# Queries and keys of a sparse-attention layer turned unsplit, compressed probabilities of two heads in one transpose, score matmuls over 512 columns

## The chip, the cores and the metric

One core of a Trainium2 chip runs the whole kernel. The metric is the device time of one execution in microseconds (us); the figure for a kernel is the median of several runs. Engines are called as in the profile: PE is the matrix engine, PEld its weight loads, DVE the vector engine, ACT the scalar engine, POOL GpSimd, SP the engine that here only issues transfers.

## What is computed

A decoder layer over 512 tokens of width 1024: a normed input is projected to pooling channels, 8 query heads of 64, six key/value slots for 2 groups, and gates. The attention part, in the reference's terms, is for each query head:

```python
s = einsum('bqgrd,bngd->bgrqn', q, kc) * scale        # 31 compressed blocks
p_cmp = masked_softmax(s, cmp_end <= t, -1);  o_cmp = p_cmp @ vc
s = einsum('bqgrd,bgqkld->bgrqkl', q, ksel) * scale   # selected blocks (all 8 of 8 here)
o_sel = masked_softmax(s, ...) @ vsel
s = einsum('bqgrd,bkgd->bgrqk', q, kw) * scale        # window of 512
o_win = masked_softmax(s, ...) @ vw
o = g0 * o_cmp + g1 * o_sel + g2 * o_win
```

q and the keys are normed and rotated first. The pooled and the attention outputs are projected, gated, added to the input, and a gated conv-MLP of inner width 2816 follows. All in float32.

## The kernel before

**Split numbers.** To keep float32 accuracy, an operand is split into a high part (float32r, written by ACT) and a low part (the rest, a DVE subtraction), in `split` (L424), and products are made as high*high + high*low + low*high. For queries and keys the two parts lie on the 128 partitions, 64 rows each: one matmul over 128 rows adds two of the products, and two matmuls, with the key tile `KT[0, ...]` and `KT[1, ...]`, add all four.

**A planner sets the order.** Every instruction is noted in a `Plan` with a price, and `emit` (L374) replays the notes in an order found by a list scheduler: up to 12 tries, of which the one with the least modelled time is written out. Each engine then works through its list in that fixed order. PE has two streams: `m` (attention) and `f` (projections of pooling channels and gates, `feature`, L705), and takes from `f` when `m` has nothing ready. `pl.behind(op)` only delays the planner's start of an operation until `op` is done; it is no wait on the chip. SBUF pages of 128x512 come from one pool of `PAGES` (L51). PSUM has 2 banks `mm` (stream f), 3 banks `tr`, one `av`, one double one `sc`.

**Turning q and k.** `rope_split(t)` (L653) rotates the 8 query heads and the 4 key heads (2 branches x 2 groups) of token block t (128 tokens), and splits them: `qs` holds, per head, 64 high and 64 low columns; `ks` holds the key's high part twice (`ks[0]`) and its low part twice (`ks[1]`). `qk_transpose(t)` (L678) turns each head's 128x128 tile on PE: 8 transposes for q and 8 for k per block, in groups of four to a PSUM bank, and ACT copies each bank to `QT` or `KT` as float32r. `turned[t]` (L700) is the last operation of block t; the rotation of block t+2, the loads of `w1` (L806) and `poolw`, and the clearing of `kcz` and `PZ` are put behind it.

**Scores.** `scores(h, i)` (L912): for query block i of head h and each key block j up to i, two matmuls of 256 columns (two branches x 128 keys).

**Compressed branch.** `cmp_scores` (L870) uses a block-diagonal `kcz` as the fixed operand and 512 columns of `QT`. `cmp_softmax` (L880) leaves `cst`: per head and block 32 high, 32 low and 32 high columns (96). `cmp_transpose(g, i)` (L901) turns the four heads of a group for block i, 4 transposes per call, 8 calls, and ACT copies 96 rows to `PTc`. `av` (L959) multiplies with `vst`, 96 rows x 64.

**Afterwards.** `PTc`'s and `cst`'s memory is taken over in the MLP by the tiles `th` (`tt`, `t2`, L1079). The MLP's 18 calls of `up_fast` (L1209) load weights (`r`), make low parts by an accumulating transfer from POOL (`sl`, `split_by_dma`, L1084), and multiply.

Of the kernel before, what the change touches and what calls it, by code (L numbers as in the profile page):

```python
# [9 lines left out]
F32R = mybir.dt.float32r  # L10
# [37 lines left out]
    CST[_n] = (_o, _o + _w)  # L48
    _o += _w
NCST = _o  # L50
PAGES = 54  # L51
RINGS = {"wraw": 3, "whi": 3, "wlo": 3}
PLAIN = 4
DIRECT = (0, 3)
# [342 lines left out]
def hybrid_layer(ctx: ExitStack, tc: tile.TileContext, xT, pos, par, cst, poolw, w1, wa, wb, wf,  # L397
# [9 lines left out]
    def f32(ap):  # L407
        return ap.bitcast(F32)

    def page(name, shape=(P, T), dt=F32):  # L410
        return pl.tile(sb, shape, dt, name, "pg", PAGES)

# [5 lines left out]
    def keep(name, shape, dt=F32, bufs=1):  # L418
        return pl.tile(sb, shape, dt, name, "t_" + name, bufs)
# [55 lines left out]
    def C(n):  # L475
        return cs[:, CST[n][0]:CST[n][1]]
# [142 lines left out]
    for t in range(NT):  # L619
# [11 lines left out]
        with pl.behind(sines):  # L631
# [2 lines left out]
                                 op1=ALU.subtract)  # L634
        vv[t] = v
    b_done = pl.last()
    vg = keep("vg", (P, H, NT))
    DVE.tensor_scalar(gates, gates, 1.0, 0.5, op0=ALU.add, op1=ALU.mult)
    DVE.tensor_mul(vg, gates[:, :, 0::3].rearrange("p t h -> p h t"),
                   C("valid")[:, None, :].to_broadcast([P, H, NT]))  # L640

    def rope_on(x, tmp, idx, n):
        np_ = x.shape[0]
# [4 lines left out]
        DVE.tensor_mul(x[:, :, 0:16], x[:, :, 0:16], ct[:, None, :].to_broadcast([np_, n, 16]))  # L648
        DVE.tensor_add(x[:, :, 0:16], x[:, :, 0:16], tmp)

    qsp, ksp = [], []

    def rope_split(t):  # L653
        x, y = qp[t], kp[t]
        DVE.tensor_mul(x[:, :, 0:16], x[:, :, 0:16], gq[:, None, :].to_broadcast([P, 8, 16]))
        y4 = y.rearrange("p (b g) d -> p b g d", b=2)
        DVE.tensor_mul(y4, y4, gkv[:, 1:3][:, :, None, :].to_broadcast([P, 2, 2, DH]))
        tmp = page("rt", (P, 12, 16))
        rope_on(x, tmp[:, 0:8], t, 8)
        rope_on(y, tmp[:, 8:12], t, 4)  # L660
        qs = [page("qs", (P, 4, 2, DH), F32R) for _ in range(2)]
        ks = [page("ks", (P, 4, 2, DH), F32R) for _ in range(2)]
        for g in range(2):
            split(qs[g][:, :, 0], qs[g][:, :, 1], x[:, 4 * g:4 * g + 4])
        kx = y[:, :, None, :].to_broadcast([P, 4, 2, DH])
        split(ks[0], ks[1], kx)
        qsp.append(qs)
        ksp.append(ks)

    for t in range(NT):  # L670
        x, y = qp[t], kp[t]
# [3 lines left out]
    pl.span = [pl.last().i, 0]  # L675
    QT, KT = {}, {}

    def qk_transpose(t):  # L678
        for g in range(2):
            pt = bank("tr", (P, 4, P))  # L680
            with pl.unit():
                for i in range(4):
                    PE.transpose(pt[:, i], f32(qsp[t][g][:, i].rearrange("p a d -> p (a d)")), ident)
            QT[g, t] = page("qt", (P, 4, P), F32R)
            ACT.activation(QT[g, t], pt, AF.Copy)
        for s in range(2):
            pt = bank("tr", (P, 2, 2, P))
            with pl.unit():
                for g in range(2):
                    for b in range(2):  # L690
                        PE.transpose(pt[:, g, b], f32(ksp[t][s][:, 2 * b + g].rearrange("p a d -> p (a d)")), ident)
            KT[s, t] = page("kt", (P, 2, 2, P), F32R)
            ACT.activation(KT[s, t], pt, AF.Copy)

    rope_split(0)
    rope_split(1)
    turned = []
    for t in range(NT):
        qk_transpose(t)
        turned.append(pl.last())  # L700
        if t + 2 < NT:
            with pl.behind(turned[t]):
                rope_split(t + 2)

    def feature(i, hi, lo):  # L705
        wh, wl = weights(flat(wf[i]), 1024)
# [136 lines left out]
        for z in kcz.values():  # L843
            POOL.memset(f32(z), 0.0)
    pk = compress_out(1)
    vst = keep("vst", (96, 2, DH), F32R)
    for g in range(2):
        src = pk[g * 32:(g + 1) * 32, 0:64]
        for s in range(2):
            ACT.activation(vst[s * 32:(s + 1) * 32, g], src, AF.Copy, scale=0.5)  # L850
        DVE.scalar_tensor_tensor(vst[64:96, g], src, 0.5, f32(vst[g * 32:(g + 1) * 32, g]),
                                 op0=ALU.mult, op1=ALU.subtract)

    def compress_kt():
        pt = bank("tr")
# [9 lines left out]
                               AF.Copy)  # L865

    cps, cst_ = {}, {}
    PTc = {g: pl.tile(sb, (96, 4, T), F32R, "ptc", "ptc", 1) for g in range(2)}

    def cmp_scores(g):  # L870
        pt = bank("tr")
        for i in range(NT):
            with pl.unit():
                for s in range(2):
                    PE.matmul(pt, kcz[s, g][:, i], QT[g, i].rearrange("p a b -> p (a b)"), start=(i == 0 and s == 0),
                              stop=(i == 3 and s == 1))
        cps[g] = page("cs", (P, 4, P))
        ACT.activation(cps[g].rearrange("p a b -> p (a b)"), pt, AF.Copy)

    def cmp_softmax(g):  # L880
        pt = bank("tr", (P, 4, P))
        with pl.unit():
            for hh in range(4):
                PE.transpose(pt[:, hh], cps[g][:, hh], ident)
        e = page("ce", (P, 16, 32))
        e4 = e.rearrange("p (h t) n -> p h (t n)", h=4)
        sm = keep("csm", (P, 3, 16), bufs=2)
        st = cst_[g] = keep("cst", (P, 16, 3, 32), F32R)
        DVE.tensor_add(e4, pt, C("cmask")[:, None, :].to_broadcast([P, 4, P]))
        DVE.tensor_reduce(sm[:, 0], e, axis=AX, op=ALU.min)  # L890
        DVE.tensor_sub(e, e, sm[:, 0][:, :, None].to_broadcast([P, 16, 32]))
        ACT.activation(e, e, AF.Exp, scale=-1.0)
        DVE.tensor_reduce(sm[:, 1], e, axis=AX, op=ALU.add)
        DVE.reciprocal(sm[:, 2], sm[:, 1])
        DVE.tensor_mul(sm[:, 2], sm[:, 2], vg[:, 4 * g:4 * g + 4].rearrange("p h t -> p (h t)"))
        DVE.tensor_mul(e, e, sm[:, 2][:, :, None].to_broadcast([P, 16, 32]))
        ACT.activation(st[:, :, 0], e, AF.Copy)
        ACT.activation(st[:, :, 2], e, AF.Copy)
        DVE.tensor_sub(st[:, :, 1], e, f32(st[:, :, 0]))

    def cmp_transpose(g, i):  # L901
        pt = bank("tr", (P, 4, P))
        with pl.unit():
            for hh in range(4):
                PE.transpose(pt[0:96, hh], f32(cst_[g][:, 4 * hh + i].rearrange("p a n -> p (a n)")), ident)
        ACT.activation(PTc[g][:, :, i * P:(i + 1) * P], pt[0:96], AF.Copy)

    Pt, PT, po, Oraw = {}, {}, {}, {}
    Oh = [page("oh", dt=F32R) for _ in range(4)]
# [2 lines left out]
    def scores(h, i):  # L912
        g, hh = divmod(h, 4)
        n = i + 1
        pt = bank("sc", (P, 4, 2, P)) if n > 2 else bank("tr", (P, 2, 2, P))
        with pl.unit():
            for j in range(n):
                for s in range(2):
                    PE.matmul(pt[:, j], QT[g, i][:, hh], KT[s, j][:, g], start=(s == 0 and j % 2 == 0),
                              stop=(s == 1), skip_group_check=True)  # L920
        sm = keep("asm", (P, 4, 2), bufs=4)
        if n > 2:
            pp = [pl.tile(sb, (P, T), F32, "pp", "pp", 10)[:, :n * P].rearrange("p (j k) -> p j k", k=P) for _ in range(2)]
        else:
            x = pl.tile(sb, (P, T), F32, "pp", "pp", 10).rearrange("p (b j k) -> p b j k", b=2, k=P)
            pp = [x[:, b, :n] for b in range(2)]
        for b in range(2):
            DVE.tensor_tensor_reduce(out=pp[b], in0=pt[:, 0:n, b], in1=mask[:, NT - n:NT], scale=1.0,
                                     scalar=3.0e38, op0=ALU.add, op1=ALU.min, accum_out=sm[:, 0, b:b + 1])
        for b in range(2):  # L930
            ACT.activation(pp[b], pp[b], AF.Exp, bias=sm[:, 0, b:b + 1], scale=-1.0,
                           accum_out=sm[:, 1, b:b + 1])
        DVE.reciprocal(sm[:, 2], sm[:, 1])
        DVE.tensor_mul(sm[:, 3], sm[:, 2], gates[:, i, 3 * h + 1:3 * h + 3])
        for b in range(2):
            DVE.tensor_scalar_mul(pp[b], pp[b], sm[:, 3, b:b + 1])
            Pt[h, b, i] = pp[b]
# [21 lines left out]
    def av(h, b):  # L959
# [4 lines left out]
        o = po[h]  # L964
        parts = [(0, 0, 0, 0), (1, 0, 1, 128), (2, 256, 2, 256), (2, 0, 3, 256)]
        if b == 1:
            PE.matmul(o[0:64], vst[:, g], PTc[g][:, h % 4], start=False, stop=False)
            parts = parts[::-1]
        for r, s, j, t0 in parts:
            n = 512 - t0  # L970
# [29 lines left out]
    cmp_softmax(0)  # L1000
    scores(0, 2)
    scores(0, 3)
    extra = {(0, 2 * i + 2): (lambda i=i: cmp_transpose(0, i)) for i in range(NT)}
    extra.update({(4, 2 * i): (lambda i=i: cmp_transpose(1, i)) for i in range(NT)})
    extra[2, 6] = lambda: cmp_softmax(1)
    for h in range(H):
        def nxt(i):
# [68 lines left out]
    H2 = T // 2  # L1076
    nh, nl, th, tl = {}, {}, {}, {}
    yh, yl = [None] * KF, [None] * KF
    tt = pl.tile(sb, (P, 4, T), F32R, "th", "ptc", 1)  # L1079
    t2 = pl.tile(sb, (P, 3, T), F32R, "th", "t_cst", 1)  # L1080
    t3 = [pl.tile(sb, (P, T), F32R, n, "t_" + n, 1) for n in ("oraw", "ot")]
    b11 = [[pl.tile(sb, (P, T), F32R, "nh", "pt", 6) for _ in range(2)] for _ in range(2)]

# [5 lines left out]
    def halves(k):  # L1089
# [13 lines left out]
        DVE.tensor_sub(tb[:, :H2], b2[:, H2:], b1[:, H2:])  # L1103
        DVE.scalar_tensor_tensor(tb[:, H2:], ta[:, H2:], -1.0, b2[:, :H2], op0=ALU.mult, op1=ALU.subtract)
        for i, x in ((0, ta), (1, tb)):
            th[k, i] = tt[:, k] if i == 0 else t2[:, k] if k < 3 else t3[0]
            tl[k, i] = page("tl", dt=F32R) if k or i else t3[1]
            (split_by_dma if i else split)(th[k, i], tl[k, i], x)

# [282 lines left out]
```

## Time and profile before

| | |
|---|---|
| time, median of 3 runs | 702.31 us (701.93 to 702.53) |
| span of the profiled execution, first to last instruction | 700.4 us |
| its own time | not listed; its span lies 1.9 us under the median of the runs |
| PE busy | 693.4 us, 4142 matmuls |
| DVE, ACT, POOL busy | 479.5, 433.4, 103.3 us |

"Busy" is the union of the instructions' spans. A matmul's span holds a pipeline tail of some 0.16 us (a 512-column one is 0.39 us long while the next one starts 0.23 us after it), so the cost of one matmul in a row of them is the distance between starts, not the span. Almost every line of the profile is L393, the line that replays the notes, so operations are told apart by the tiles they write and read: `tr<-cs,qs` is a transpose into a `tr` bank of the tile `qs` with the identity in `cs`.

### The profile page before, as it was taken

Reading aid. Unit: us, or ns where it says so; the run is one execution under the profiler, and the core shown is the slowest. Engines: PE = TensorE matmul, PEld = TensorE weight load, DVE = VectorE, ACT = ScalarE, POOL = GpSimd, SP = SyncE. Lnnn points to the kernel's source line nnn. Section 1 sums busy time; section 2 is a strip of 40 time slices with the busy share of each in tenths; the row PEclk is TensorE's granted clock in tenths of the full one; section 3 lists DMA queues with packets and bytes.
Section 4 is the critical chain, followed back from the end, with each engine's and each line's share of the span. In section 5 each row is a group of like instructions: output and inputs, shape, how many; then the busy total and the mean of one; then the engine's idle time right before and its main releaser. Section 6 shows DMA issues by size and latency. Waiting matters only on the chain.

```text
span 700.4 us, 11319 instructions
## 1 busy us (share of the span) xinstructions
PE 693.4 (99%) x4142; PEld 612.7 (87%) x4142; DVE 479.5 (68%) x1024; ACT 433.4 (62%) x792; POOL 103.3 (15%) x127
## 2 busy tenths in 40 slices
PE   9999999999999999999999999999999999999997
PEld 8898888888888888888888898999999999999986
DVE  6768488777866653685559876776777867675542
ACT  8567378766776663343358766776776766675320
POOL 0011310010011010000012232222322222121000
PEclk9999999999999999999999999999999999999999
DMA  8468342555565557844468887897787887774131
GB/s 296 141 162 246 89 121 76 135 140 131 122 166 146 156 128 204 306 159 139 159 140 201 191 175 172 203 208 181 176 177 185 192 207 187 178 177 104 45 129 60
DMA packets 45271, 113.99 MB, mean 163 GB/s; under 512 B 5280, under 2 KB 5408, under 8 KB 45216
## 3 DMA queue, kind: packets, MB, share of 16 engines
q1 hardware_dynamic: 29232, 76.57, 33.9%
q0 software_dynamic: 15840, 36.71, 28.9%
q8 instruction: 32, 0.52, 0.3%
q14 instruction: 23, 0.19, 0.1%
q10 hardware_dynamic: 144, 0.01, 0.0%
HBM read 70.27 MB, written 6.29 MB: 109 GB/s over the span
## 4 chain that ended last, share of the span: by engine, by line
PE 94%; issue 2%; DMA 1%; DVE 1%; POOL 1%; ACT 0%; POOLq 0%; ACTq 0%
PE mm L393 41%; PE tr L393 30%; PE sc L393 13%; PE av L393 11%; DMA sl<-r 1%; POOL sl L393 0%; POOL tl L393 0%; DVE kc L393 0%; DVE th L393 0%; DVE qs L393 0%; DVE o L393 0%; DVE ks L393 0%; ACT qs L393 0%; POOLq L393 0%; POOL ones L393 0%
## 5 line engine op out<-in xcount | busy, mean ns | idle before, releaser
L393 ACT ACTIVATE whi<-wraw 128x1024 fp32r<-128x1024 f32 (+1 forms) x96 | 97.9, 1021 | 71.5 <-issue 27.2
L393 DVE TENSOR_TENSOR wlo<-wraw,whi 128x1024 fp32r<-128x1024 f32 (+1 forms) x66 | 76.3, 1157 | 16.9 <-ACT whi L393 15.4
L393 POOL DMA_DIRECT2D wlo<-wraw x30 | 26.0, 868 | 336.1 <-ACT wlo L393 272.6
L393 PE MATMUL mm<-xh,whi 128*128 128x512 f32 x176 | 73.4, 417 | 0.3
L393 PE MATMUL mm<-xl,whi 128*128 128x512 f32 x176 | 69.0, 392 | 0.0
L393 PE MATMUL mm<-xh,wlo 128*128 128x512 f32 x176 | 69.0, 392 | 0.0
L393 PE MATMUL mm<-tl,sh 128*128 128x256 f32 x190 | 53.5, 282 | 0.0
L393 PE MATMUL mm<-th,sl 128*128 128x256 f32 x174 | 49.1, 282 | 0.0
L393 PE MATMUL mm<-th,sh 128*128 128x256 f32 x174 | 49.0, 281 | 0.0
L393 POOL DMA_DIRECT2D sl<-r x36 | 31.0, 862 | 115.9 <-ACT sl L393 71.9
L393 ACT ACTIVATE pp<-pp,asm 128x384 f32<-128x384 f32 (+3 forms) x64 | 35.4, 556 | 11.5 <-DVE asm L393 11.4
L393 ACT ACTIVATE wlo<-wraw 128x1024 fp32r<-128x1024 f32 x30 | 31.7, 1058 | 14.9 <-PE mm L393 6.9
L393 PE MATMUL sc<-yh,whi 128*128 128x512 f32 x104 | 40.5, 389 | 0.0
L393 PE MATMUL sc<-yl,whi 128*128 128x512 f32 x104 | 40.5, 389 | 0.0
L393 PE MATMUL sc<-yh,wlo 128*128 128x512 f32 x104 | 40.5, 389 | 0.0
L393 PEld LDWEIGHTS mm<-xh,wlo 128*128 128x128 f32 x176 | 33.0, 188 | 7.5
L393 PEld LDWEIGHTS mm<-xh,whi 128*128 128x128 f32 x176 | 33.2, 189 | 5.8 <-DVE th L393 1.0
L393 DVE SCALAR_TENSOR_TENSOR ft<-fg,pr,ft 128x511 f32<-128x511 f32 (+1 forms) x44 | 32.9, 749 | 7.1 <-ACT ft L393 6.4
L393 PEld LDWEIGHTS mm<-xl,whi 128*128 128x128 f32 x176 | 33.3, 189 | 3.6
L393 PEld LDWEIGHTS mm<-tl,sh 128*128 128x128 f32 x190 | 35.7, 188 | 0.4
L393 PEld LDWEIGHTS mm<-th,sh 128*128 128x128 f32 x174 | 32.7, 188 | 1.1
L393 PEld LDWEIGHTS mm<-th,sl 128*128 128x128 f32 x174 | 32.7, 188 | 0.0
(397 smaller groups left out, 2095.4 us busy)
## 6 DMA issues: line engine op xcount, KB each, us to landing
wlo<-wraw POOLq DMA_DIRECT2D x30, 512.0 KB, 4.6
wraw<-wup SPq DMA_DIRECT2D x26, 512.0 KB, 4.0
wraw<-wf SPq DMA_DIRECT2D x22, 512.0 KB, 3.4
r<-wup SPq DMA_DIRECT2D x36, 256.0 KB, 5.7
sl<-r POOLq DMA_DIRECT2D x36, 256.0 KB, 5.2
wraw<-wdn SPq DMA_DIRECT2D x16, 512.0 KB, 4.2
sl<-s POOLq DMA_DIRECT2D x18, 256.0 KB, 5.7
sl<-wraw POOLq DMA_DIRECT2D x18, 256.0 KB, 5.9
```

The source lines that it names most:

```text
L393: getattr(self.real[o.eng], method)(*a, **kw)
```

## The change

Queries and keys stay unsplit until they are turned. `rope_split` becomes `rope_qk`, without splits. `qk_transpose(t)` turns two heads (2 x 64 columns) at a time in float32: 4 transposes for q, 2 for k. From the PSUM bank, `halves_of` writes the high part of a head's 64 rows with ACT and the low part into the other 64 rows with DVE. `QT` is now by head parity r, `KT` by a pair of key blocks a and group g. `KT[1]` is `KT[0]` with its two halves of partitions swapped, made by two transfers of 64 partitions x 256 columns (64 KB) on SP's queue, per block and group: 16 in all, each waiting for the split before it. `turned[t]` is now the last of these transfers.

`scores` takes two key blocks per matmul (512 columns) where it can. `cmp_scores` is two matmuls of 256 columns in place of each one of 512, as the heads of a group lie in two `QT` tiles. `cst` holds 32 high and 32 low columns per head and block, a pair of heads is turned together (`cmp_transpose(g, r)`, 4 transposes per call, 4 calls), `vst` has 128 rows x 128 per parity of the pair, zero outside its own, and is written by 8 ACT and 4 DVE instructions instead of 4 and 2. There are 56 pages instead of 54; three `th` tiles of the MLP take pages.

```diff
--- before.py
+++ after.py
@@ -48,7 +48,7 @@
...
 NCST = _o
-PAGES = 54
+PAGES = 56
...
@@ -634,10 +634,11 @@
...
     b_done = pl.last()
-    vg = keep("vg", (P, H, NT))
+    vg = keep("vg", (P, 2, 2, NT, 2))
     DVE.tensor_scalar(gates, gates, 1.0, 0.5, op0=ALU.add, op1=ALU.mult)
-    DVE.tensor_mul(vg, gates[:, :, 0::3].rearrange("p t h -> p h t"),
-                   C("valid")[:, None, :].to_broadcast([P, H, NT]))
+    for g in range(2):
+        DVE.tensor_mul(vg[:, g], gates[:, :, 12 * g:12 * g + 12:3].rearrange("p t (k r) -> p r t k", r=2),
+                       C("valid")[:, None, :, None].to_broadcast([P, 2, NT, 2]))
     def rope_on(x, tmp, idx, n):
...
@@ -648,9 +649,7 @@
...
-    qsp, ksp = [], []
-
-    def rope_split(t):
+    def rope_qk(t):
...
@@ -658,14 +657,6 @@
...
         rope_on(y, tmp[:, 8:12], t, 4)
-        qs = [page("qs", (P, 4, 2, DH), F32R) for _ in range(2)]
-        ks = [page("ks", (P, 4, 2, DH), F32R) for _ in range(2)]
-        for g in range(2):
-            split(qs[g][:, :, 0], qs[g][:, :, 1], x[:, 4 * g:4 * g + 4])
-        kx = y[:, :, None, :].to_broadcast([P, 4, 2, DH])
-        split(ks[0], ks[1], kx)
-        qsp.append(qs)
-        ksp.append(ks)
...
@@ -675,32 +666,42 @@
...
+    def halves_of(dst, c, src):
+        o = 64 - c
+        ACT.activation(dst[c:c + 64], src, AF.Copy)
+        DVE.tensor_sub(dst[o:o + 64], src, f32(dst[c:c + 64]))
+
     def qk_transpose(t):
+        pt = bank("tr", (P, 4, P))
+        with pl.unit():
+            for i in range(4):
+                PE.transpose(pt[:, i], qp[t][:, 2 * i:2 * i + 2].rearrange("p a d -> p (a d)"), ident)
+        for r in range(2):
+            QT[r, t] = page("qt", (P, 4, P), F32R)
+            halves_of(QT[r, t], 64 * r, pt[64 * r:64 * r + 64])
+        pt = bank("tr", (P, 2, P))
+        with pl.unit():
+            for b in range(2):
+                PE.transpose(pt[:, b], kp[t][:, 2 * b:2 * b + 2].rearrange("p a d -> p (a d)"), ident)
+        a, j = divmod(t, 2)
         for g in range(2):
-            pt = bank("tr", (P, 4, P))
-            with pl.unit():
-                for i in range(4):
-                    PE.transpose(pt[:, i], f32(qsp[t][g][:, i].rearrange("p a d -> p (a d)")), ident)
-            QT[g, t] = page("qt", (P, 4, P), F32R)
-            ACT.activation(QT[g, t], pt, AF.Copy)
-        for s in range(2):
-            pt = bank("tr", (P, 2, 2, P))
-            with pl.unit():
-                for g in range(2):
-                    for b in range(2):
-                        PE.transpose(pt[:, g, b], f32(ksp[t][s][:, 2 * b + g].rearrange("p a d -> p (a d)")), ident)
-            KT[s, t] = page("kt", (P, 2, 2, P), F32R)
-            ACT.activation(KT[s, t], pt, AF.Copy)
-
-    rope_split(0)
-    rope_split(1)
+            if j == 0:
+                for s in range(2):
+                    KT[s, a, g] = page("kt", (P, 2, 2, P), F32R)
+            k0, k1 = (KT[s, a, g][:, j] for s in range(2))
+            halves_of(k0, 64 * g, pt[64 * g:64 * g + 64])
+            for c in (0, 64):
+                SP.dma_start(f32(k1[c:c + 64]), f32(k0[64 - c:128 - c]))
+
+    rope_qk(0)
+    rope_qk(1)
...
             with pl.behind(turned[t]):
-                rope_split(t + 2)
+                rope_qk(t + 2)
     def feature(i, hi, lo):
...
@@ -843,13 +844,17 @@
...
     pk = compress_out(1)
-    vst = keep("vst", (96, 2, DH), F32R)
+    vst = keep("vst", (P, 2, 2, P), F32R)
+    with pl.behind(turned[2]):
+        POOL.memset(f32(vst), 0.0)
...
         src = pk[g * 32:(g + 1) * 32, 0:64]
-        for s in range(2):
-            ACT.activation(vst[s * 32:(s + 1) * 32, g], src, AF.Copy, scale=0.5)
-        DVE.scalar_tensor_tensor(vst[64:96, g], src, 0.5, f32(vst[g * 32:(g + 1) * 32, g]),
-                                 op0=ALU.mult, op1=ALU.subtract)
+        for a in range(2):
+            v, o = vst[:, g, a], 64 * a
+            for s in range(2):
+                ACT.activation(v[o + 32 * s:o + 32 * s + 32, 0:64], src, AF.Copy, scale=0.5)
+            DVE.scalar_tensor_tensor(v[o:o + 32, 64:128], src, 0.5, f32(v[o:o + 32, 0:64]),
+                                     op0=ALU.mult, op1=ALU.subtract)
     def compress_kt():
...
@@ -865,15 +870,18 @@
...
     cps, cst_ = {}, {}
-    PTc = {g: pl.tile(sb, (96, 4, T), F32R, "ptc", "ptc", 1) for g in range(2)}
+    PTc = {g: pl.tile(sb, (P, 2, T), F32R, "ptc", "ptc", 1) for g in range(2)}
     def cmp_scores(g):
...
                 for s in range(2):
-                    PE.matmul(pt, kcz[s, g][:, i], QT[g, i].rearrange("p a b -> p (a b)"), start=(i == 0 and s == 0),
-                              stop=(i == 3 and s == 1))
+                    for r in range(2):
+                        PE.matmul(pt[:, r * 256:(r + 1) * 256], kcz[s, g][:, i],
+                                  QT[r, i][:, 2 * g:2 * g + 2].rearrange("p a b -> p (a b)"),
+                                  start=(i == 0 and s == 0 and r == 0), stop=(i == 3 and s == 1),
+                                  skip_group_check=True)
...
@@ -883,27 +891,29 @@
...
         e = page("ce", (P, 16, 32))
-        e4 = e.rearrange("p (h t) n -> p h (t n)", h=4)
+        e5 = e.rearrange("p (r t k) n -> p r k t n", r=2, t=NT)
+        cm = C("cmask").rearrange("p (t n) -> p t n", t=NT)[:, None].to_broadcast([P, 2, NT, 32])
         sm = keep("csm", (P, 3, 16), bufs=2)
-        st = cst_[g] = keep("cst", (P, 16, 3, 32), F32R)
-        DVE.tensor_add(e4, pt, C("cmask")[:, None, :].to_broadcast([P, 4, P]))
+        st = cst_[g] = keep("cst", (P, 16, 2, 32), F32R)
+        for r in range(2):
+            DVE.tensor_add(e5[:, r], pt[:, 2 * r:2 * r + 2].rearrange("p k (t n) -> p k t n", t=NT), cm)
...
         DVE.reciprocal(sm[:, 2], sm[:, 1])
-        DVE.tensor_mul(sm[:, 2], sm[:, 2], vg[:, 4 * g:4 * g + 4].rearrange("p h t -> p (h t)"))
+        DVE.tensor_mul(sm[:, 2], sm[:, 2], vg[:, g].rearrange("p r t k -> p (r t k)"))
...
         ACT.activation(st[:, :, 0], e, AF.Copy)
-        ACT.activation(st[:, :, 2], e, AF.Copy)
...
-    def cmp_transpose(g, i):
-        pt = bank("tr", (P, 4, P))
+    def cmp_transpose(g, r):
+        pt = bank("tr", (P, NT, P))
+        st = cst_[g].rearrange("p (r t k) a n -> p r t (k a n)", r=2, t=NT)
         with pl.unit():
-            for hh in range(4):
-                PE.transpose(pt[0:96, hh], f32(cst_[g][:, 4 * hh + i].rearrange("p a n -> p (a n)")), ident)
-        ACT.activation(PTc[g][:, :, i * P:(i + 1) * P], pt[0:96], AF.Copy)
+            for i in range(NT):
+                PE.transpose(pt[:, i], f32(st[:, r, i]), ident)
+        ACT.activation(PTc[g][:, r], pt.rearrange("p a b -> p (a b)"), AF.Copy)
...
@@ -914,10 +924,11 @@
...
         with pl.unit():
-            for j in range(n):
+            for j in range(0, n, 2):
+                m = min(2, n - j)
                 for s in range(2):
-                    PE.matmul(pt[:, j], QT[g, i][:, hh], KT[s, j][:, g], start=(s == 0 and j % 2 == 0),
-                              stop=(s == 1), skip_group_check=True)
+                    PE.matmul(pt[:, j:j + m], QT[h % 2, i][:, h // 2], KT[s, j // 2, g][:, :m], start=(s == 0),
+                              stop=(s == 1))
...
@@ -964,7 +975,7 @@
...
         if b == 1:
-            PE.matmul(o[0:64], vst[:, g], PTc[g][:, h % 4], start=False, stop=False)
+            PE.matmul(o, vst[:, g, h // 2 % 2], PTc[g][:, h % 2], start=False, stop=False)
...
@@ -1000,8 +1011,8 @@
...
     scores(0, 3)
-    extra = {(0, 2 * i + 2): (lambda i=i: cmp_transpose(0, i)) for i in range(NT)}
-    extra.update({(4, 2 * i): (lambda i=i: cmp_transpose(1, i)) for i in range(NT)})
+    extra = {(0, 4 * r + 2): (lambda r=r: cmp_transpose(0, r)) for r in range(2)}
+    extra.update({(4, 4 * r): (lambda r=r: cmp_transpose(1, r)) for r in range(2)})
...
         def nxt(i):
@@ -1076,8 +1087,10 @@
...
     yh, yl = [None] * KF, [None] * KF
-    tt = pl.tile(sb, (P, 4, T), F32R, "th", "ptc", 1)
-    t2 = pl.tile(sb, (P, 3, T), F32R, "th", "t_cst", 1)
+    tt = [pl.tile(sb, (P, 2, T), F32R, "th", "ptc", 1)]
+    tt = [tt[0][:, k] for k in range(2)] + [page("th", dt=F32R) for _ in range(2)]
+    t2 = pl.tile(sb, (P, 2, T), F32R, "th", "t_cst", 1)
+    t2 = [t2[:, k] for k in range(2)] + [page("th", dt=F32R)]
...
@@ -1103,7 +1116,7 @@
...
         for i, x in ((0, ta), (1, tb)):
-            th[k, i] = tt[:, k] if i == 0 else t2[:, k] if k < 3 else t3[0]
+            th[k, i] = tt[k] if i == 0 else t2[k] if k < 3 else t3[0]
...
```

## Rows read from the trace of the kernel before

**Rows 1.** The profile's page: busy time of the engines over the span (share of the span, instructions), and of the 40 slices of the span the busy tenths of PE and the granted clock of PE in tenths.
```profile
PE 693.4 (99%) x4142; PEld 612.7 (87%) x4142; DVE 479.5 (68%) x1024; ACT 433.4 (62%) x792; POOL 103.3 (15%) x127
...
PE   9999999999999999999999999999999999999997
...
PEclk9999999999999999999999999999999999999999
```

**Rows 2.** The view of waits, PE alone, whole run: who was waited for, us in total, times, longest us.
```profile
PE tr L393 <- DMA sl<-r: 1.4, 1, 1.4
PE mm L393 <- POOL ones L393: 1.0, 1, 1.0
PE tr L393 <- ACT qt L393: 0.2, 1, 0.2
```

**Rows 3.** Busy time in stretches of the span (us; instructions behind the x): the turning of q and k, the compression of keys and values, a part of the attention, and the main part of the MLP's fast calls. Columns: stretch, its length, PE, PEld, DVE, ACT, POOL, granted clock, share of the transfer engines, GB/s.
```profile
52.00:75.00 23.00, 22.51 (x139) 19.08 (x138) 19.81 (x65) 17.89 (x35) 5.36 (x8) 1.00 0.81 226
75.00:93.00 18.00, 18.00 (x113) 15.49 (x112) 7.96 (x32) 4.31 (x14) 5.20 (x8) 1.00 0.30 69
...
98.00:150.00 52.00, 51.90 (x299) 44.30 (x297) 42.55 (x137) 39.04 (x86) 4.41 (x6) 1.00 0.46 115
...
424.00:640.00 216.00, 215.77 (x1559) 204.55 (x1560) 156.24 (x235) 152.63 (x276) 55.18 (x64) 1.00 0.79 183
```

**Rows 4.** The chain that ended last, in order of time, at the end of the attention (start us, length us, what).
```profile
271.25 14.28 PE mm L393 x63
```

**Rows 5.** The same chain while the last block of q and k is turned.
```profile
69.76 0.42 ACT qs L393
...
70.20 0.76 DVE qs L393 x2
70.96 0.33 DVE kc L393
71.29 0.60 DVE ks L393
...
73.27 1.66 PE mm L393 x6
```

**Rows 6.** Groups of PE's instructions, shapes kept apart: those that the change touches (busy us, mean ns of one span).
```profile
L393 PE MATMUL sc<-kt,qt 128*128 128x256 f32 x112 | 16.1, 283 | 0.0
...
L393 PE MATMUL tr<-kt,qt 128*128 128x256 f32 x48 | 8.6, 287 | 0.0
...
L393 PE MATMUL tr<-cs,cst 128*96 128x128 f32 x32 | 4.8, 272 | 0.0
L393 PE MATMUL tr<-cs,ks 128*128 128x128 f32 x32 | 4.7, 274 | 0.2 <-ACT qt L393 0.2
...
L393 PE MATMUL tr<-cs,qs 128*128 128x128 f32 x32 | 4.5, 273 | 0.1
```

**Rows 7.** PE's instructions in order of time, merged where alike (start us, us from the first start to the last end).
```profile
62.31 1.04 PE L393 MATMUL tr<-cs,ks 128*128 128x128 f32 x8
...
70.23 0.40 PE L393 MATMUL mm<-xh,wlo 128*128 128x512 f32 x1
...
93.30 3.81 PE L393 MATMUL tr<-qt,kcz 128*128 128x512 f32 x16
...
100.64 1.12 PE L393 MATMUL sc<-kt,qt 128*128 128x256 f32 x8
101.60 0.40 PE L393 MATMUL mm<-xh,whi 128*128 128x512 f32 x1
...
109.90 0.60 PE L393 MATMUL tr<-cs,cst 128*96 128x128 f32 x4
```

**Rows 8.** Groups of ACT's and of DVE's instructions, shapes kept apart: those that the change removes, and those nearest to what it adds.
```profile
L393 ACT ACTIVATE ot<-av 64x512 f32<-64x512 f32 x8 | 4.8, 596 | 8.3 <-PE av L393 8.2
...
L393 ACT ACTIVATE kt<-tr 128x512 fp32r<-128x512 f32 x8 | 4.6, 599 | 0.9 <-PE tr L393 0.9
...
L393 ACT ACTIVATE qs<-qp 128x256 fp32r<-128x256 f32 x8 | 2.9, 413 | 0.3 <-DVE qp L393 0.3
L393 ACT ACTIVATE ks<-kp 128x512 fp32r<-128x512 f32 x4 | 2.5, 629 | 1.0 <-DVE kp L393 1.0
...
L393 DVE TENSOR_TENSOR pt<-tr,pt 128x512 fp32r<-128x512 f32 x16 | 11.0, 688 | 4.0 <-ACT pt L393 3.7
...
L393 DVE TENSOR_TENSOR kc<-mm,rb 64x256 f32<-64x256 f32 x8 | 3.4, 422 | 0.1
L393 DVE TENSOR_TENSOR qs<-qp,qs 128x256 fp32r<-128x256 f32 x8 | 3.2, 420 | 2.4 <-ACT qs L393 2.4
L393 DVE TENSOR_TENSOR ks<-kp,ks 128x512 fp32r<-128x512 f32 x4 | 2.7, 685 | 0.1
```

**Rows 9.** Transfers issued in the whole run: instruction, times, KB each, median us from issue to landing. `w<-w` is the load of `w1`.
```profile
w<-w SPq DMA_DIRECT2D x8, 256.0 KB, 6.2
...
out<-o SPq DMA_DIRECT2D x8, 256.0 KB, 2.0
```

**Rows 10.** PE's instructions that read the keys first, and the last copy of a key (the view of tile `kt`: duration ns min/median/max, first and last start us).
```profile
L393 PE MATMUL tr<-kt,qt x48: 274/282/387, 92.3 to 251.9; 128*128 128x256 f32 x48
L393 ACT ACTIVATE kt<-tr x8: 588/600/614, 57.1 to 73.3; 128x512 fp32r<-128x512 f32 x8
```

**Rows 11.** Who SP's queue waited for between 440 and 640 us, in the MLP's fast calls.
```profile
SPq L393 <- DMA sl<-wraw: 111.5, 15, 11.6
```

## Prediction

> **What bounds the kernel now.** I read the page first. PE is busy for 99% of the span, in every slice but the last, and the granted clock is at its upper level, 2.4 GHz, throughout [rows 1]. A busy PE can still be a PE that waits inside its pipeline, so I read PE's waits next: over the whole run it waits 1.4 us for a transfer, 1.0 us at the very start and 0.2 us for ACT [rows 2]. The table by stretches says the same for each stage: PE is full, DVE and ACT have room in most, but DVE is at 19.8 of 23.0 us while q and k are turned [rows 3]. The chain that ended last goes through PE. So a matmul taken away should move the end by what it cost, unless a new wait takes its place.
>
> Two more views tell how safe that is. After the last attention matmul PE still runs 14.3 us of stream f alone [rows 4]: the attention may be late by that much before the end sees it, provided PE can run f's matmuls in the meantime. And there is one weak place in the stretch that is changed: PE's last matmul before the last block of q and k starts at 70.23 and holds PE until about 70.46; f goes on only at 73.27 [rows 5, 7]. Sixteen transposes fill 1.76 us of those 2.81 (price below), so 1.05 us are lost to a chain over ACT's and DVE's splits and the emptying of f's bank (`kc`).
>
> **PE's work, part by part.** Prices are distances between starts. Eight transposes take 1.04 us from the first start to the last end, one is 0.274 long: (1.04 - 0.274)/7 = 0.109 us each, say 0.110 [rows 6, 7]. The four compressed ones give (0.60 - 0.272)/3 = 0.109 [rows 6, 7]. Sixteen 512-column matmuls take 3.81 us, (3.81 - 0.39)/15 = 0.228 each [rows 7]; eight of 256 columns take 0.96 us to the next start, 0.120 each [rows 7].
> - q and k: 32 + 32 transposes [rows 6] become 16 + 8. 40 x 0.110 = 4.40 us off.
> - Compressed probabilities: 32 [rows 6] become 16. 16 x 0.109 = 1.74 us off.
> - Scores: per head 20 matmuls of 256 columns (112 + 48 = 160 in all [rows 6]) become 8 of 512 and 4 of 256, so 64 pairs become one each: 64 x (0.240 - 0.228) = 0.77 us off. The columns stay, so this is small.
> - `cmp_scores`: 16 of 512 become 32 of 256: 16 x 0.012 = 0.19 us on.
> - `av` with `vst`: 8 matmuls of 512 columns before and after; only rows that hold zeros are added. Nothing.
>
> Sum: 4.40 + 1.74 + 0.77 - 0.19 = 6.7 us off. Unchanged waits put the profiled span at 700.4 - 6.7 = 693.7. The time has 1.9 us around the span, to which nothing is added: 702.3 - 6.7 = 695.6.
>
> One rule speaks against the second item. The four compressed transposes, which load 96 columns, are spaced like the others [rows 7]. The Trainium skill (TensorE: Matmul & The Clock Gate, LDWEIGHTS) gives a weight load of P columns P/1.2 ns, 80 for 96 columns and 107 for 128; by that, loads that set the pace would make the old narrow transposes cheaper than the new ones. The trace doesn't agree on the pace. What it would do to the time is the fifth rival.
>
> **The other engines where q and k are turned (52 to 75 us).** ACT loses 8 x 0.413 + 4 x 0.629 of splits and 16 copies of 0.6, some 15.4 us, and gains 8 copies of 64x512 (nearest 0.596) and 8 of 64x256 (nearest 0.413), 8.1 us [rows 8]: 7.3 us lighter. DVE loses 8 x 0.420 + 4 x 0.685 = 6.1 us and gains 8 subtractions of 64x512 from PSUM (nearest 0.688) and 8 of 64x256 (nearest 0.422), 8.9 us [rows 8]: 2.8 us heavier, and 19.8 + 2.8 leaves 0.4 of 23 [rows 3]. DVE also empties f's banks, as seen at 70.96 [rows 5], so this is the tightest place after the change. A `tr` bank is now held through two ACT copies and two subtractions instead of one copy.
> PE has 4.4 us less of its own in this stretch. If f steps in, nothing is lost; cover is f's stock of 14.3 us [rows 4]. Bounds: the 1.05 us lost now goes away since ACT is lighter (-1.05), or all the freed time stays empty (+4.4). I take zero: PE's only wait here is 0.2 us now [rows 2], and it waits on the same ACT and DVE work.
>
> **The swapped keys.** Sixteen transfers of 64 KB on SP's queue, two per block and group, each waiting for a split; behind them stand the loads of `w1`, `poolw` and f's weights. No row has such a transfer; 256 KB ones land 2.0 us (quiet) to 6.2 us (in this very stretch) after issue [rows 9]. The last key is copied at 73.3 + 0.6, the first reader starts at 92.3 [rows 10]: 18 us of cover, so price zero; without cover, up to 6.2. As `turned[t]` is now such a landing, the planner puts the rotation of block t+2 behind it: two links in a row (0 to 2, 1 to 3), 4 to 12.4 us later in the order. Cover: again f's 14.3 us.
>
> **Small items at zero.** `vst` gets 4 more ACT and 2 more DVE instructions, `vg` one more; they fall between 75 and 93 us, where ACT works 4.3 and DVE 8.0 of 18 us [rows 3]. `cmp_softmax` drops an ACT copy per group and splits one DVE addition into two halves; `cmp_transpose` drops four ACT evictions; ACT has 13 us of room there [rows 3]. The clearing of `vst` is one more POOL instruction while POOL is 5.4 of 23 busy [rows 3].
>
> **Pages.** 56 minus three for `th` leaves the MLP 53 instead of 54. In the MLP SP's queue waits 111 us for weight buffers (`sl<-wraw` lets go of one) [rows 11], so buffers, more than pages, set when loads start: price zero. Bounds: the one wait of 1.4 us there [rows 2] goes, or it comes in more of the 18 calls. The planner starts afresh on the whole order, so this wait may move either way.
>
> **Rivals.**
> 1. The freed time in the turning stretch stays empty: 695.6 + 4.4 = 700.0. For it: DVE full, f's banks emptied by DVE. Against: f has stock and ACT is lighter. Chance 0.13.
> 2. Slower: the two links put the turning later by 12.4 us, and f can't fill because its weight loads stand behind the waiting swaps in SP's queue. 695.6 + 12.4 = 708.0; it is slower than before once more than 6.7 us stay empty. For it: transfer engines at 0.81 in this stretch [rows 3]. Against: weights are bought ahead, and the loads wait for buffers anyway. Chance 0.06.
> 3. The missing page delays each of the 18 `up_fast` calls by 0.3 us: 5.4 us, 701.0. For it: such a wait exists once. Against: PE is full there, 215.8 of 216.0 [rows 3]. Chance 0.05.
> 4. The change doesn't shorten PE's list, or the freed time was never on the path: 702.3. Against: 99% [rows 1]. Chance 0.03.
> 5. Weight loads set a transpose's price by columns: the old 32 cost 0.109 x 96/128 = 0.082 each, 2.62 us, the new 16 cost 1.74: 0.87 off instead of 1.74, 696.5. Against: 0.60 us for four of either width. Chance 0.03. It is the rule of the Trainium skill's page above.
>
> **How the numbers follow.** The forecast, 695.6, has the remaining 0.70. Range: its lower end has both known waits gone, 695.6 - 1.05 - 1.4 = 693.1; the upper end takes in rival 1, 700.0. That leaves out rivals 2, 3 and 4, and some of the forecast's tails. A measurement of this kernel can tell 0.2%, 1.4 us, from no change, so faster is below 700.9: forecast, rivals 1 and 5, and a little of 3: 0.87. Within 0.2%: rival 4 and most of 3: 0.07. Slower: 0.06.
>
> **What would show it.** Right: PE's matmuls fall from 4142 to 4142 - 40 - 16 - 64 + 16 = 4038; score matmuls of 512 columns stand 0.228 apart; PE's waits stay near 2.6 us; f's tail after the attention is no shorter by more than what the window lost. Wrong, by step: transposes further apart than 0.110 (a price); gaps of PE between 52 and 80 us with DVE or a `tr` bank as releaser (rival 1) or a weight load as releaser (rival 2); more waits for `sl<-r` after 400 us (rival 3); first readers of `kt` waiting for a transfer (the cover of 18 us). The forecast is wrong outright if PE's gaps in the turning stretch grow by several us.

## The result and the profile after

| | before | changed |
|---|---|---|
| time, median | 702.17 us (701.93 to 702.53, 4 runs) | 695.99 us (695.29 to 698.37, 4 runs) |
| span of the profiled execution | 700.4 us | 693.6 us (its own time 695.46) |
| matmuls | 4142 | 4038 |

The ratio is 0.9917, 95% interval 0.9899 to 0.9935: 4.6 to 7.1 us off. In a later comparison the same kernel gave 0.9923 (0.991 to 0.9936). The forecast was 695.6, and 693.7 for the span. That the span comes out within 0.1 us is luck: a second execution of the same kernel, e1_after's, spans 694.9 us. One of the four runs, 698.37, had a mean granted clock of 0.995 where the others had 0.999 or more; the last section comes back to it.

The page of the changed kernel, its lines of busy time and of PE's slices and clock, answer to [rows 1]:

```profile
PE 685.8 (99%) x4038; PEld 604.1 (87%) x4038; DVE 483.2 (70%) x1033; ACT 424.3 (61%) x778; POOL 103.5 (15%) x128
...
PE   9999999999999999999999999999999999999997
...
PEclk9999999999999999999999999999999999999999
```

PE still fills the span; it is busy for 7.6 us less. The groups of PE's instructions in the changed kernel, shapes kept apart, answer to [rows 6] (busy us, mean ns of one span):

```profile
L393 PE MATMUL sc<-kt,qt 128*128 128x512 f32 x48 | 13.7, 393 | 0.8 <-DVE asm L393 0.8
...
L393 PE MATMUL tr<-kt,qt 128*128 128x512 f32 x16 | 5.2, 403 | 0.0
...
L393 PE MATMUL tr<-cs,cst 128*128 128x128 f32 x16 | 2.4, 272 | 0.0
L393 PE MATMUL tr<-cs,qp 128*128 128x128 f32 x16 | 2.4, 272 | 0.0
...
L393 PE MATMUL tr<-cs,kp 128*128 128x128 f32 x8 | 1.6, 276 | 0.9 <-DVE kp L393 0.9
```

And PE in order of time, as in [rows 7]:

```profile
53.35 0.60 PE L393 MATMUL tr<-cs,qp 128*128 128x128 f32 x4
...
72.04 0.39 PE L393 MATMUL mm<-xh,wlo 128*128 128x512 f32 x1
73.38 0.41 PE L393 MATMUL tr<-cs,kp 128*128 128x128 f32 x2 [0.94 <-DVE kp L393]
...
92.19 4.00 PE L393 MATMUL tr<-qt,kcz 128*128 128x256 f32 x32
...
99.70 1.07 PE L393 MATMUL sc<-kt,qt 128*128 128x512 f32 x4
...
107.72 0.60 PE L393 MATMUL tr<-cs,cst 128*128 128x128 f32 x4
109.12 0.93 PE L393 MATMUL sc<-kt,qt 128*128 128x512 f32 x4 [0.80 <-DVE asm L393]
```

Four transposes of q take 0.60 us, (0.60 - 0.272)/3 = 0.109 each, as before. So do four of the widened compressed ones. The 32 halves of `cmp_scores` stand (4.00 - 0.283)/31 = 0.120 apart, and the four 512-column score matmuls at 99.70 stand (1.07 - 0.393)/3 = 0.226 apart. Where the price of a matmul was needed, the old price holds.

PE's waits in the changed kernel, whole run, against [rows 2]:

```profile
PE mm L393 <- POOL ones L393: 1.0, 1, 1.0
PE tr L393 <- DVE kp L393: 0.9, 1, 0.9
PE sc L393 <- DVE asm L393: 0.8, 1, 0.8
PE tr L393 <- DMA sl<-r: 0.8, 1, 0.8
```

They add up to 3.5 us against 2.6, so the forecast's sign that they stay near 2.6 did not come. The wait for a transfer in the MLP is shorter; one of 0.9 for DVE stands where q and k are turned, and one of 0.8 at the first attention scores after the compressed softmax.

The table by stretches, for the turning and for the compression, against [rows 3]:

```profile
52.00:75.00 23.00, 22.06 (x121) 18.48 (x121) 20.94 (x63) 14.00 (x24) 5.27 (x5) 1.00 0.76 196
75.00:93.00 18.00, 18.00 (x111) 15.36 (x110) 11.78 (x45) 5.67 (x17) 6.36 (x12) 1.00 0.80 223
```

DVE fills 20.9 of 23 us while q and k are turned, and part of its work has moved behind 75 us (11.8 there instead of 8.0). ACT is 3.9 us lighter in the first stretch, where the forecast had 7.3; DVE is 1.1 us heavier there, where it had 2.8, and 3.8 heavier behind it. The chain of what ended last shows the same from PE's side, and at its end that stream f's tail is untouched, 14.28 us as in [rows 4]:

```profile
71.32 0.68 DVE qt L393
72.02 0.70 DVE qt L393
72.74 0.24 DVE kp L393
73.00 0.24 DVE kp L393
...
264.68 14.28 PE mm L393 x63
```

The last two rotations of a key (`kp`) stand in DVE's queue behind two low parts of q (`qt`), and PE waits for them. Before, the loss in this place ran over ACT's and DVE's splits [rows 5]; now it runs over DVE alone. It was also spread over several gaps between PE's instructions, each partly under the tail of the matmul before it, as these lines of the kernel before show:

```profile
71.67 0.60 PE L393 MATMUL tr<-cs,ks 128*128 128x128 f32 x4
72.48 0.66 PE L393 MATMUL tr<-cs,ks 128*128 128x128 f32 x4 [0.20 <-ACT qt L393]
```

Four transposes are worth 0.44 us, but the next four start 0.81 later: 0.37 are lost, and the view of waits counts only 0.20 of it. So of the 0.9 us by which the waits grew, 0.7 is the same loss in one gap, now seen (0.9 instead of 0.2), and not new time.

The keys' swaps, from the view of tile `kt` (duration ns min/median/max, first and last start; the time to landing stands in its last line), against [rows 9, 10]:

```profile
L393 PE MATMUL tr<-kt,qt x32: 278/388/481, 90.5 to 244.0; 128*128 128x256 f32 x16, 128*128 128x512 f32 x16
L393 SPq DMA_DIRECT2D kt<-kt x16: 461/470/1282, 55.9 to 82.3; - x16
...
DMA to landing us min/median/max: 1.9/5.0/8.4
```

A swap of 64 KB took 5.0 us in the middle and up to 8.4, though the forecast's bounds for it went to 6.2. The last one is issued at 82.3, 8 us before the first matmul that reads any key, at 90.5. No row of PE's waits names one, so the cover held, with less to spare than the 18 us reckoned.

### The profile page after: what moved, and what is told of

Same layout as the page of the kernel before. It is cut to its first block, busy times and chain, and to the rows that moved or that the text cites. A ratio compares the mean times of both kernels' runs of the same rounds, so it can differ in the third digit from the quotient of the medians.

```text
span 693.6 us, 11113 instructions
## 1 busy us (share of the span) xinstructions
PE 685.8 (99%) x4038; PEld 604.1 (87%) x4038; DVE 483.2 (70%) x1033; ACT 424.3 (61%) x778; POOL 103.5 (15%) x128
## 4 chain that ended last, share of the span: by engine, by line
PE 86%; DMA 4%; DVE 4%; issue 4%; ACT 1%; POOL 1%; POOLq 0%; ACTq 0%; DVEq 0%; SPq 0%
PE mm L393 37%; PE tr L393 27%; PE sc L393 12%; PE av L393 10%; DMA sl<-r 4%; DMA r<-wup 1%; POOL sl L393 1%; DVE ft L393 0%; DVE qt L393 0%; DVE kp L393 0%; DVE qp L393 0%; DVE kt L393 0%; DVE th L393 0%; ACT whi L393 0%; DVE wlo L393 0%
```

## The experiments

All were timed in five rounds beside the kernel before. Theory: the time follows PE's list; each matmul is worth the distance between starts, and waits add what the profile shows. Rivals: a lucky order gave the gain; DVE leaves PE spare time in the turning stretch; the links over the swaps cost time; the missing pages cost time.

**e1_after**: the changed kernel again. 

> The changed kernel itself, as the measure for the three beside it. By price (every matmul taken off PE's list is worth the distance between starts) it stands 6.7 us under the kernel before, 695.5. By the rival that a lucky order gave the gain, nothing is foretold beyond its own earlier time, 695.3 to 698.4 us.

Measured: 696.26 us (694.9 to 698.67, 6 runs), before 701.78. One run of the six, 698.67, had a mean granted clock of 0.995. PE's waits in its trace, whole run:

```profile
PE mm L393 <- ACT u L393: 1.0, 1, 1.0
PE mm L393 <- POOL ones L393: 1.0, 1, 1.0
PE tr L393 <- DVE kp L393: 0.9, 1, 0.9
PE tr L393 <- DMA sl<-r: 0.9, 1, 0.9
PE sc L393 <- DVE asm L393: 0.8, 1, 0.8
```

The wait of 1.0 for `u`, in the MLP, is not in the first trace of the same kernel: executions of one kernel differ by such a wait.

**e1_turn16**: 40 transposes come back.

```diff
-            for i in range(4):
+            for i in (0, 1, 2, 3) * 2:
                 PE.transpose(pt[:, i], qp[t]...
...
-            for b in range(2):
+            for b in (0, 1) * 4:
                 PE.transpose(pt[:, b], kp[t]...
```

> Each block of q and k is turned with 16 transposes again instead of 6: the q transposes are made twice and the k transposes four times, into the same place, so that 40 transposes come back and nothing else changes. By price: 40 x 0.110 = 4.4 us slower than the changed kernel, about 699.9. By the rival that DVE bounds the turning stretch and PE has time to spare there: less than 3.4 us, since the 1.0 us that PE now waits there is filled first, and down to none.

Measured: 699.03 us (698.03 to 699.37), 2.8 us over e1_after. That is the rival's side of the line. Its waits of PE, whole run:

```profile
PE mm L393 <- POOL ones L393: 1.0, 1, 1.0
PE mm L393 <- DVE kc L393: 0.6, 1, 0.6
PE tr L393 <- DVE kp L393: 0.3, 1, 0.3
PE tr L393 <- ACT whi L393: 0.2, 1, 0.2
```

The wait for `kp` fell from 0.9 to 0.3, but 0.6 came for `kc` next to it, so the turning stretch gave only a little. The waits of 0.8 for `asm`, 0.9 for `sl<-r` and 1.0 for `u`, which e1_after's trace has, are gone. PE is busy for 690.0 us against 686.1, so 3.9 of the price stand in its list, and its waits are 2.5 us shorter; together that is 1.4 of the 1.5 us between the two profiled spans. What is missing from the price in these traces is waits far from the edit that went when the planner started afresh, and not spare time of PE where q and k are turned.

**e1_scores256**: two key blocks per matmul become one each.

```diff
-                    PE.matmul(pt[:, j:j + m], QT[h % 2, i][:, h // 2], KT[s, j // 2, g][:, :m], ...
+                    PE.matmul(pt[:, j], QT[h % 2, i][:, h // 2], KT[s, j // 2, g][:, j % 2], ...
```

> The score matmuls go back to 256 columns, 64 more of them over the same columns; all else as changed. By price: 64 x 0.012 = 0.8 us slower than the changed kernel (0.5 by the spacing in the MLP). By the rival that wide matmuls matter by themselves (a wide one keeps PE better fed): 2 us or more. By a lucky order: any change of sign.

Measured: 696.78 us (695.08 to 699.3), 0.5 over e1_after. The sign and size fit the price, but the runs of each spread over 4 us, so this alone does not show it.

**e1_cmp_twice**: `for i in (0, 1, 2, 3) * 2` in `cmp_transpose`. 

> Each transpose of compressed probabilities is made twice into the same place: 16 transposes come back, nothing else changes. By price: 16 x 0.110 = 1.8 us slower than the changed kernel. By the rule that a transpose's cost goes with the loaded columns, also 1.8, so it tells the price of a 128-column one alone. By a lucky order: not tied to 1.8.

Measured: 696.49 us (695.35 to 702.7, 9 runs), 0.2 over e1_after: not the price. Three of the nine runs had clocks of 0.987 to 0.995. Its profiled run has 16 more matmuls and three PE waits of 2.6 us together, against five of 4.6 in e1_after's: what the list gained, other waits lost. Inconclusive for the price in the time. On PE itself the price shows:

```profile
107.78 1.04 PE L393 MATMUL tr<-cs,cst 128*128 128x128 f32 x8
```

Eight take 1.04 us, (1.04 - 0.272)/7 = 0.110 each.

**e2_before53**: the kernel before with `PAGES = 53`. 

> The kernel before with 53 pages instead of 54, the number that the changed kernel leaves to the MLP; nothing else. If pages set when the MLP's loads start: SP's queue waits there for matmuls that give pages back, PE's waits after 400 us grow, and the time by 0.5 to 2 us over the kernel before. If the waits seen in the changed kernel's MLP are an accident of a fresh order: within 0.3 us, and no such waits of SP.

Measured: ratio 1.0014 (1.0005 to 1.0022), 702.85 against 701.98 us. Between 440 and 640 us SP's queue now waits for matmuls that give pages back, which in the kernel before it did for 0.3 us:

```profile
SPq L393 <- PE mm L393: 7.1, 5, 3.1
```

The changed kernel's trace has 7.8 us of it too. So with a page less, and the order planned afresh, the kernel before takes about 0.9 us longer, and SP's queue feels the page in the MLP. That PE does is not shown: its waits after 400 us are 1.0 for `sl<-r` and 0.5 for `u`, 1.5 against 1.4 before, and a new one of 0.7 for `pz` lies in the attention.

**e2_after54**: the changed kernel with `PAGES = 54`. 

> The changed kernel with 54 pages, so that its MLP has 51. If pages set it: PE's waits after 400 us grow from 1 to 2 us to more than 3, and the time by 1 to 4 us over the changed kernel (696.3). If an accident of the order: no trend, 695 to 697.

Measured: 699.21 us (696.44 to 704.18, 12 runs), 2.9 over e1_after. Nine of the twelve runs had a mean clock of 0.987 to 0.998 and took 698.3 to 704.2; the three at 1.000 took 696.4, 697.7 and 697.7. So about half of the 2.9 us goes with the clock. The rest isn't traced: the profiled run is the slowest of the twelve, and in it PE's only wait after 400 us is 0.2, so the reason given in the expectation does not show. Its table by stretches shows where the clock fell:

```profile
60.00:72.00 12.00, 12.00 (x58) 9.65 (x57) 11.29 (x34) 7.71 (x12) 4.40 (x4) 1.00 0.75 172
72.00:76.00 4.00, 2.80 (x25) 2.78 (x25) 3.82 (x9) 2.76 (x4) 1.92 (x2) 0.98 1.04 283
76.00:93.00 17.00, 17.00 (x64) 15.09 (x63) 6.33 (x26) 0.96 (x3) 3.77 (x7) 0.50 0.68 192
93.00:98.00 5.00, 5.00 (x24) 3.63 (x22) 2.61 (x10) 2.73 (x4) 1.41 (x5) 1.00 0.00 0
```

PE in order of time in the same run:

```profile
73.25 0.41 PE L393 MATMUL tr<-cs,kp 128*128 128x128 f32 x2 [1.20 <-DVE kp L393]
73.49 4.88 PE L393 MATMUL tr<-kcb,w 128*128 128x62 f32 x32
...
79.56 0.63 PE L393 MATMUL mm<-xh,whi 128*128 128x512 f32 x1
79.99 0.63 PE L393 MATMUL mm<-xl,whi 128*128 128x512 f32 x1
```

After the wait for `kp`, 1.2 us here, come 32 matmuls of 62 columns, and in them the granted clock falls to 0.50, from 2.4 to 1.2 GHz, and stays there until 93 us. A 512-column matmul takes 0.43 us from start to start instead of 0.23. PE made 64 matmuls from 76 to 93 us where the changed kernel made 102. This run took 6.5 us more than the two at 697.7 us that kept the clock.

The same place in e1_cmp_twice's profiled run warns against calling the wait the whole cause:

```profile
73.47 0.41 PE L393 MATMUL tr<-cs,kp 128*128 128x128 f32 x2 [1.16 <-DVE kp L393]
73.72 3.81 PE L393 MATMUL tr<-kcb,w 128*128 128x62 f32 x32
```

There 1.16 us of waiting and the same 32 matmuls went by at 2.4 GHz.

**e2_no_rotation**: without `rope_on` for q and the two branches' keys. 

> The changed kernel without the rotation of q and of the two branches' keys (8 DVE instructions per block, some 1.65 us each block); the rotation of the compressed keys stays. If DVE bounds the turning stretch: PE's wait there for the keys' rotation (0.9 us) is gone and the time falls by 1.0 us, or a little more. If the order sets it: the wait stays within 0.3 us.

Measured: 695.01 us (694.17 to 695.56), 1.25 under e1_after. No wait for `kp` is left among PE's waits, and the loss at the last keys falls from 1.1 us to 0.25 (68.00 to 68.48 in its trace, for a matmul of 0.23): the rotations in DVE's queue were the cause of that wait. The time shows it less clearly, as the interval (0.9885 to 0.9918) overlaps that of e1_after and the waits for `asm` (0.8) and `u` (1.0, now 0.4) shrank in the same trace.

**e2_link** and **e3_link**: the links are cut.

```diff
             halves_of(k0, 64 * g, pt[64 * g:64 * g + 64])
+            split_done[t] = pl.last()
...
-        turned.append(pl.last())
+        turned.append(split_done[t])
```

> The changed kernel with turned[t] set to the split of the last key instead of its swap's landing, so that the planner may start the rotation of block t+2 and the loads behind it earlier. By the forecast (stream f covers): the same within 0.5 us, with the turning ended earlier. By the second rival (links and swaps hold up the turning): PE's wait of 0.9 us at 73 us goes and the time falls by 1 us or more.

> The changed kernel with turned[t] at the split of the last key (the kernel of e2_link), as the measure for the three beside it: 694.1 again, every run within 1 us of it, granted clock 0.999 or more in each, since PE's wait of 0.9 us at 73 us is 0.2 here. If the 694.1 was an accident of that chip: 695 to 697 with single runs at 698 and more.

Measured: 694.11 us (693.15 to 694.5), ratio 0.9891 (0.9876 to 0.9905), and in the next comparison 694.06 us (693.67 to 694.32), ratio 0.9884 (0.9869 to 0.9899). It is the best version of this study, about 2 us under the changed kernel both times. Every one of the eight runs had a clock of 0.999 or more. The waits of PE in e3_link:

```profile
PE mm L393 <- POOL ones L393: 1.0, 1, 1.0
PE tr L393 <- DVE kp L393: 0.4, 1, 0.4
PE tr L393 <- ACT ptc L393: 0.2, 1, 0.2
PE tr L393 <- DMA sl<-r: 0.2, 1, 0.2
```

The wait for `kp` is halved (in e2_link it is 0.2), those for `asm` and `u` are gone, and that for `sl<-r` is 0.2. Together PE waits 1.8 us against 4.6 in e1_after's trace, which accounts for 2.8 of the 2.9 us between the two spans. Here the forecast (no cost for the links) was wrong by some 2 us.

**e3_link_turn16**: e3_link with the edit of e1_turn16. 

> That kernel with the 40 transposes of q and k made again, into the same places. By price, now that no wait stands in the way: 40 x 0.110 = 4.4 us slower than e3_link, 698.5. If PE's freed time in the turning stretch is partly empty whatever the links: less than 3.4 us.

Measured: 697.91 us (697.47 to 698.25), 3.85 over e3_link. That lies between the price (4.4) and the rival's bound (3.4). PE is busy for 690.1 us in it and for 686.0 in e3_link, 4.1 apart for 40 transposes, 0.103 each; what the list gained fell just short of the price, and most of it reached the end.

**e3_link_all_back**: e3_link with the edits of e1_turn16, e1_scores256 and e1_cmp_twice together. 

> All matmuls that the change takes off are given back: 40 transposes of q and k, 16 of compressed probabilities (each made twice), and score matmuls of 256 columns. PE's list is then as long as before, and 16 longer for cmp_scores. By price: 4.4 + 1.8 + 0.8 = 6.9 us slower than e3_link, 701.0, so level with the kernel before (702.0) within 1 us. If the gain came from somewhere else than PE's list (lighter ACT, fewer banks, order): it stays at least 2 us under the kernel before.

Measured: 701.5 us (700.0 to 702.34, 11 runs), 7.4 over e3_link; ratio to the kernel before 0.9989 (0.998 to 0.9997). Everything else of the change but the links is in this kernel: lighter ACT, swaps, `tr` banks held longer, fewer pages for the MLP. What is left of the gain is 0.75 us. PE's list carries the rest.

**e3_link_act**: e3_link with the swaps issued by `ACT.dma_start`. 

> The kernel of e3_link with the 16 swaps of keys issued from ACT's queue instead of SP's, so that no weight load stands behind a swap. By the forecast (swaps are hidden where they are): the same as e3_link within 0.5 us. By the second rival (swaps hold up SP's loads): 0.5 to 1.5 us faster.

Measured: 694.04 us (693.55 to 694.14), the same as e3_link. So the swaps in SP's queue cost e3_link nothing, whatever weight loads stand behind them.

## Why the prediction was right

**PE's list, 6.7 us.** This term was right. The count of matmuls came out as said, 4038, the spacings are unchanged, and the profiled span fell by 6.8. Taking the losses at waits out of the spans of three traces (the changed kernel, e1_after, e3_link) leaves about 7 us for the list; that is an estimate, which adds to each wait the 0.16 us of tail that hides part of it and takes 1.05 us for the turning before. The whole list given back costs 7.4 us (e3_link_all_back), its largest term alone 3.85 of the 4.4 forecast (e3_link_turn16). Of the smaller terms (compressed probabilities, scores) only the sum with the rest is shown in the time; each alone disappears under waits that move when the planner orders afresh (e1_scores256, e1_cmp_twice).

**The turning stretch at zero.** The forecast took the loss of 1.05 us there as unchanged. The profile bears it out: the gap from 72.04 to 73.38 is 1.34 us for a matmul of 0.23, so 1.1 us are lost, now for DVE alone, as its extra load suggested. e2_no_rotation shows that the rotations in DVE's queue are the cause. A gap with DVE as releaser was the forecast's own sign for the first rival; it came, but no larger than the loss before. PE's freed time did not stay empty: e1_turn16 and e3_link_turn16 return 2.8 and 3.85 us of it, so the first rival (all of 4.4 lost) falls. The reason given for zero, that PE waits on the same ACT and DVE work, held only for DVE's part; that the loss kept its size when ACT left the path is partly luck.

**The swapped keys at zero.** Right for the transfers themselves (e3_link_act; no reader waits). Wrong for the links. "Cover: again f's 14.3 us" held for f's stock, which ended as long as before, but cutting the links gave 2 us (e2_link, e3_link). That was no lack of f's matmuls and no blocked weight load, as the second rival had it. It was shorter waits for `kp`, `asm`, `sl<-r` and `u`; the clock, which stayed up in all these runs, adds little, since the other five runs of e1_after have a median of 696.1. A link is no wait on the chip and acts only through the planner's order. How much of the 2 us is the earlier rotation and how much the order elsewhere can't be split from these runs; the wait for `kp` alone is 0.5.

**Pages at zero.** The third rival's 5.4 us falls: the changed kernel's waits after 400 us are 0.8 and 1.9 in its two traces, 1.4 before. The term may be mis-sized by up to 0.9 us (e2_before53), inside the range; that this is the page and not the new order isn't shown, and e2_after54, where half of the excess goes with the clock, doesn't settle it.

**The rule on weight loads** in the Trainium skill (TensorE: Matmul & The Clock Gate, LDWEIGHTS), the fifth rival, doesn't set the pace: four compressed transposes with 128 loaded columns take 0.60 us in the changed kernel, as four with 96 did [rows 7].

The measured median is 0.4 and 0.7 us above the forecast in the two comparisons. A new wait of 0.8 for `asm` in both traces, waits such as the 1.0 for `u` that come in one execution and not in another, and single runs at a lower clock pull it up; the forecast had none of them.

## What to carry to other kernels

Where PE is full and another stream of matmuls waits to be run, cost an edit by the distance between starts of the matmuls it removes, and check it by giving them back: made twice into the same place, they change nothing else but the planned order. Small terms vanish under waits that an automatic order moves about, so test the sum rather than each. Waits in a list of waits can also be the same loss in another shape: compare distances between starts there too. When a change makes a tight place tighter, look at what follows the wait: here a wait of one microsecond ahead of 62-column matmuls was followed by a fall of the clock in some executions and not in others.

## What was not expected of the hardware

The granted clock fell to 1.2 GHz for some 17 us after a wait of 1.2 us that was followed by 62-column matmuls (e2_after54, profiled). The changed kernel has the same place with a wait of 0.9 us and kept 2.4 GHz in its profiled runs, and e1_cmp_twice kept it with 1.16 us. Two of the changed kernel's ten runs had a mean clock of 0.995 and took 698.4 and 698.7 us, 1.7 us or more over each of the others. That the fall was at the same place in these two is likely, not shown, as they have no trace. Over all runs, a mean clock under 0.999 came in 15 of 37 executions of the kernels whose trace shows 0.9 to 1.2 us of wait at this place (the changed kernel 2 of 10, e1_scores256 1 of 6, e1_cmp_twice 3 of 9, e2_after54 9 of 12), and in none of 37 of those with 0.7 us or less or no wait (e1_turn16, e2_no_rotation, e2_link and the four e3 kernels). So the wait goes with the fall; why one execution falls and the next does not stays open, and where in a run it fell is known from one trace alone. Transfers of 64 KB within SBUF took 1.9 to 8.4 us to land beside loads of weights, much like those of 256 KB [rows 9].
